# First mixer of a two-block transformer: projections, delta rule and attention in another order, with the residual put away in DRAM

## The chip, the core and the metric

The kernel runs on one core of one Trainium2 chip. The metric is the device time of one execution in microseconds (us); lower is better. TensorE multiplies 128x128 weights with up to 512 columns into PSUM, VectorE (DVE), ScalarE (ACT) and GpSimd (POOL) do the elementwise work, and DMA queues on SyncE (SP), ScalarE and GpSimd move data. Each engine works through its own instructions strictly in the order in which the program lists them; semaphores tie the engines together.

## The reference

The program is two blocks of a transformer on 512 tokens of width 1024. The change touches only the mixer of the first block. It computes two branches from one normalised input and one projection matrix `w_in`:

```python
proj = h @ w_in                      # 1024 -> qkv_a 1536 | z_a 512 | a, b 16 | qkv_b 1536
# branch a: gated delta rule, 4 heads of 128, forward and backward
qkv = silu(short_conv(qkv_a, conv_w))            # 5 taps along the tokens
q, k, v = l2_normalize(q), l2_normalize(k), v
lmat = strict_lower(kb @ k.T * decay)            # per chunk and head
tmat = inverse(eye + lmat)                       # triangular solve
u, w = tmat @ (v * beta), tmat @ (kb * exp(g))
for chunk: v_new = u - w @ state; o = qg @ state + intra @ v_new
           state = state * exp(gl) + kdec.T @ v_new
o_a = rms_norm(o_fwd + o_bwd) * silu(z_a)
# branch b: banded attention, 8 heads of 64, with a bias by distance
o_b = softmax(rms_norm(q_b) @ rms_norm(k_b).T + bias) @ v_b
x = x + concat(o_a, o_b) @ w_out
```

Before the mixer stands a feed-forward block, behind it another; then the second transformer (two layers) follows.

## The kernel before

Everything is kept with features on the 128 partitions and the 512 tokens along the free dimension. A projection of 128 output features is one weight block: 512 KB come by DMA into one of three `raw` buffers, ScalarE rounds them into `wh`, VectorE puts the rest into `wl` (two buffers of each), and TensorE issues 8 x 3 products `xl·wh`, `xh·wl`, `xh·wh` of 512 columns (`projF`, through `mm3`), 24 per block. `w_in` makes 28 blocks: 12 for the convolved q, k, v of the delta rule (tiles `pqkv`, from which `pad` is cut and `cv` is made by five taps; blocks 0 to 7 are q and k and are normalised by `row_scales` and `row_apply`, 8 to 11 are v), 8 for q and k of attention (`psw`, normalised and stored to DRAM as `qkd`), 4 for v of attention (`psv`, turned into `sV`) and 4 for the gate z (`psz`). `w_out` makes 8 more (`pwo`).

Between these stands the delta rule: matrices `B` and `IT` by head and direction (`pkk`, `pqk`, `pgr`), a triangular inverse of the 32x32 diagonal blocks on VectorE alone (31 pairs of instructions on `dX` and `dT`; the blocks reach it through DRAM as `dg`, `dgd`, `dM`, and leave it through `dgi` to `dR`), two levels that widen the inverse to 128x128 (`unit`: masks `bl` by GpSimd, `py`, copies `ys`, `pa`, `pb`), and the recurrence over four chunks for eight heads and directions (`psc`, `vn`, `pso`). Attention works on 32 items, one head and 128 queries each: scores `pS`, bias and maximum on VectorE, exponential `P`, transposition `ptp`, copy `PT`, product `po`, scaled into `Y`. `prepare(h)` fetches K and Q of a head from `qkd`, splits them on ScalarE and GpSimd and fetches its bias `bq` with GpSimd's queue; `bq` shares two buffers with `dM` and `dT`.

The source is written as one program, and a list scheduler places the instructions of each engine when the program is built, under the limits of buffers and PSUM banks. PSUM's eight banks are two pools of four, `acc` (projections) and `mx` (the rest). Lines that the text speaks of: L244 is every matmul, L250 and L262 elementwise work, L269 and L272 ScalarE, L623 the bias fetch, L631 the fetch `T<-qkd`.

Of the kernel before, what the change touches and what calls it, by code (L numbers as in the profile page):

```python
# [9 lines left out]
F32 = mybir.dt.float32  # L10
F32R = mybir.dt.float32r
# [7 lines left out]
NT = 512  # L19
# [186 lines left out]


class Builder:
    def __init__(self, tc, A, out, taps=None, stop=None):
# [102 lines left out]

    def wget(self, kk=8):
        nc = self.nc
        n = 128 * kk * 128
        src = self.w_ap[self.w_off:self.w_off + n].rearrange("(p x) -> p x", p=128)
        self.w_off += n
        with self.tc.high_priority():
            raw = self.ps_w.tile([128, 8, 128], F32, tag="raw", name="raw", bufs=3)
            h = self.ps_w.tile([128, 8, 128], F32R, tag="wh", name="wh", bufs=2)  # L320
            l = self.ps_w.tile([128, 8, 128], F32R, tag="wl", name="wl", bufs=2)
            nc.sync.dma_start(out=raw[:, :kk].rearrange("p k n -> p (k n)"), in_=src)
            self.acopy(h[:, :kk], raw[:, :kk])
            self.sub(l[:, :kk], raw[:, :kk], h[:, :kk].bitcast(F32))
        return h, l
# [12 lines left out]

    def projF(self, XH, XL, c0, n, name):

        h, l = self.wget()
# [5 lines left out]
    def projV(self, XH, XL, toks, name):  # L347

        c0, n = min(c for c, _ in toks), sum(k for _, k in toks)
        t = self.slab("sT", "vt")  # L350
        for ps, s in self.projF(XH, XL, c0, n, name):
            self.acopy(t[:, s], ps)
        return t
# [436 lines left out]
    def mixer1(self):  # L790
# [60 lines left out]
        def conv(m, _):  # L851
            pad = self.slab("sT", "pad")
            nc.gpsimd.memset(pad[:, 0:2], 0.0)
            nc.gpsimd.memset(pad[:, 514:516], 0.0)
            for ps, s in self.projF(XH, XL, MT, NT, "pqkv"):
# [10 lines left out]
            if m < 8:  # L866
                self.act(cv, cv, AF.Silu)
            return cv

        def sums(m, cv):  # L870
            if m >= 8:
                self.act(cv, cv, AF.Silu)
            return cv, self.row_scales(cv, chunks, 128, 1.0, self.mx) if m < 8 else None

        def rest(m, got):
            cv, y = got
            if m < 8:
                self.row_apply(cv, y, chunks, 128, 128 ** -0.5 if m < 4 else 1.0, self.mx)
            else:
                pt = self.mx("pvt")  # L880
# [14 lines left out]
        dgs = [self.slab("u", "dg", width=NT) for _ in range(2)]  # L895
        cc = [slice(128 * c, 128 * c + 128) for c in range(4)]
        by_c = lambda a: a.rearrange("p (c t) -> p c t", t=128)
        for h in range(4):
# [4 lines left out]
            for d in range(2):  # L903
# [44 lines left out]
        for d in range(2):  # L948
            for x in range(4):
                src = d2[32 * x + 16 * d:32 * x + 16 * d + 16, :].rearrange("u (r c) -> r u c", c=32)  # L950
                eng = nc.sync if x % 2 else nc.scalar
                eng.dma_start(out=R[d][32 * x:32 * x + 32, :].rearrange("p (u c) -> p u c", c=32), in_=src)
            nc.vector.transpose(out=Rt[d], in_=R[d])


# [118 lines left out]

        sw = self.small("sw", 1)
        self.ts(sw, self.v("qn"), 0.125, ALU.mult)
        qkd = self.ps_dram.tile([8, 128, NC], F32, name="qkd")

        def proj(i, _):
            group = []  # L1080
            for m in (2 * i, 2 * i + 1):
                t = self.slab("y" if m % 4 == 3 else "sT", "sT")
                for ps, s in self.projF(XH, XL, MT, NT, "psw"):
                    self.mul(t[:, s], ps, rs[:, s])
                group.append(t)
            return group

        def sums(i, group):
            return group, self.group_scales(group, SEQ, 64, 1.0 / 64, self.acc)

        def normed(i, got):
            for m, t, y in zip((2 * i, 2 * i + 1), *got):
                self.row_apply(t, y, SEQ, 64, sw if m < 4 else self.v("kn"), self.acc)
                nc.gpsimd.dma_start(out=qkd[m, :, S], in_=t[:, S])

        staged(4, proj, sums, normed)
        V = [self.slab("V", "sV", width=NT) for _ in range(4)]
        staged(4, lambda m, _: self.projV(XH, XL, toks, "psv"), lambda m, t: self.turnV(
            t, toks, lambda i, ps: self.act(V[i][:, cc[m]], ps, AF.Copy, scale=rsc[:, i:i + 1]), self.acc))


        Yh, Yl = [None] * 8, [None] * 8
        heads = {}

        def prepare(h):
            p, x = divmod(h, 2)
            r = slice(64 * x, 64 * x + 64)
            K = self.stackK(qkd[4 + p, r, :], S, ("sT", "u"), False)
            Q = self.stackQ(qkd[p, r, :], S, ("sT", "u"), False)
            heads[h] = {"K": K, "Q": Q, "Y": heads[h - 1]["Y"] if x else self.slab("y", "Y", width=NT),  # L1110
# [3 lines left out]
        def scores(i, _):  # L1114
# [19 lines left out]
        def turn(i, P):  # L1134
            T = self.slab("u", "PT", width=NT)
            pt = self.mx("ptp")
            for cs in cc:
                self.tr(pt[:, cs], P[:, cs])
            self.acopy(T, pt)
            return T  # L1140

        def product(i, T):
# [3 lines left out]
            z = slice(t, t + 1)  # L1146
            po = self.mx("po")
            for j, cs in enumerate(cc):
# [3 lines left out]
            if t == 3 and x:  # L1152
                Yh[4 + p], Yl[4 + p] = self.slab("u", "Yh", F32R), self.slab("u", "Yl", F32R)

# [4 lines left out]

                self.to_features(by_c(u["Y"]), None, sink, self.mx)  # L1160

        zs = [None] * 4

        def gate(m):
            zs[m] = z = self.slab("z" if m < 3 else "u", "z")
            for ps, s in self.projF(XH, XL, MT, NT, "psz"):
                self.mul(z[:, s], ps, rs[:, s])

# [9 lines left out]

        def step(i, _):
            if i in (2, 7, 12, 17):  # L1180
                gate((i - 2) // 5)
            if i in (20, 22, 24, 26):
                gated((i - 20) // 2)
            return scores(i, _)
# [553 lines left out]

    nu = 32

# [69 lines left out]
```

## Time and profile before

| | before |
|---|---|
| time, median of 3 runs | 3395.32 us (3391.58 to 3395.39) |
| time of the profiled execution | 3389.28 us |
| its span | 3387.5 us |
| granted TensorE clock, mean of the span | 0.956 |
| TensorE busy | 3264.6 us, 96% of the span |
| VectorE, ScalarE, GpSimd busy | 51%, 34%, 14% |
| the first mixer in the span | about 400 to 877 us |

Busy shares say in how much of the time an instruction was in the engine. A granted clock of 1.00 is 2.4 GHz and 0.50 is 1.2 GHz; values between are means over a stretch. In the rows, `[8.31 <-POOL Q L250]` says that the engine was idle for 8.31 us until the GpSimd instruction of line 250 that writes `Q` was done.

### The profile page before, as it was taken

What the parts mean: (1) busy time and instruction counts of PE and PEld (TensorE: products, weight loads), DVE (VectorE), ACT (ScalarE), POOL (GpSimd) and SP (SyncE); (2) the same over time, 40 slices, a digit from 0 to 9 for tenths busy, and PEclk for the clock granted to TensorE, in tenths of its full rate; (3) what the DMA queues carried; (4) which work ended last, traced back from release to release, by engine and by line L of the source; (5) the groups of instructions that cost most, each with busy time, mean ns of one, the idle gap of its engine ahead of it and who ended that gap; (6) DMA issues with size and microseconds to landing.
All of it is one profiled execution on the core that took longest, in us unless ns stands there. A gap on an engine that the chain in (4) does not pass through costs nothing.

```text
span 3387.5 us, 47666 instructions
## 1 busy us (share of the span) xinstructions
PE 3264.6 (96%) x18886; PEld 2816.5 (83%) x18886; DVE 1716.5 (51%) x3632; ACT 1145.1 (34%) x1958; POOL 480.9 (14%) x575
## 2 busy tenths in 40 slices
PE   8999989998999999999899999999999799999998
PEld 6778778876888889998898899999888688788886
DVE  4443378563544355544674744433665374654433
ACT  4222343365322233212553232222322363232221
POOL 1010010422000013321220400000342221400000
PEclk9999999998999999888998999999998898899999
DMA  3333223332333233123332522223323342523332
GB/s 127 103 106 115 87 63 106 101 96 65 93 94 94 91 112 109 60 79 103 116 117 72 164 88 90 92 95 124 97 78 95 115 126 94 165 87 97 94 94 77
DMA packets 121271, 337.26 MB, mean 100 GB/s; under 512 B 28853, under 2 KB 29248, under 8 KB 121048
## 3 DMA queue, kind: packets, MB, share of 16 engines
q1 hardware_dynamic: 87656, 267.95, 25.5%
q0 software_dynamic: 21712, 54.51, 5.2%
q10 hardware_dynamic: 11680, 11.76, 1.1%
q8 instruction: 148, 2.42, 0.3%
q14 instruction: 75, 0.61, 0.1%
HBM read 298.42 MB, written 39.56 MB: 100 GB/s over the span
## 4 chain that ended last, share of the span: by engine, by line
PE 55%; DMA 3%; DVE 2%; issue 2%; POOL 1%; ACT 1%; POOLq 0%; SPq 0%; DVEq 0%; ACTq 0%
PE pgz L244 11%; PE pd L244 7%; PE pg L244 7%; PE pu L244 7%; PE po L244 4%; PE pwo L244 3%; PE pA L244 2%; PE pqk L244 2%; DMA T<-qkd 2%; PE pod L244 2%; PE pdz L244 1%; PE pS L244 1%; PE pT L244 1%; PE pbr L244 1%; PE pdi L244 1%
## 5 line engine op out<-in xcount | busy, mean ns | idle before, releaser
L272 ACT CAST wh<-raw 128x1024 fp32r<-128x1024 f32 (+1 forms) x448 | 463.6, 1035 | 1532.1 <-issue 722.7
L250 DVE TENSOR_TENSOR wl<-raw,wh 128x1024 fp32r<-128x1024 f32 (+1 forms) x448 | 555.4, 1240 | 425.8 <-ACT wh L272 425.2
L244 PE MATMUL pg<-xl,wh 128*128 128x512 f32 (+1 forms) x880 | 283.3, 354 | 13.2 <-DVE xl L262 13.2
L244 PE MATMUL pg<-xh,wh 128*128 128x512 f32 (+1 forms) x880 | 282.4, 353 | 0.0
L244 PE MATMUL pu<-xl,wh 128*128 128x512 f32 (+1 forms) x880 | 281.3, 352 | 0.0
L244 PE MATMUL pd<-hl,wh 128*128 128x512 f32 (+1 forms) x880 | 281.1, 352 | 0.0
L244 PE MATMUL pu<-xh,wh 128*128 128x512 f32 (+1 forms) x880 | 281.0, 352 | 0.0
L244 PE MATMUL pd<-hh,wh 128*128 128x512 f32 (+1 forms) x880 | 280.8, 352 | 0.0
L244 PE MATMUL pg<-xh,wl 128*128 128x512 f32 (+1 forms) x880 | 280.5, 351 | 0.0
L244 PE MATMUL pu<-xh,wl 128*128 128x512 f32 (+1 forms) x880 | 279.7, 350 | 0.0
L244 PE MATMUL pd<-hh,wl 128*128 128x512 f32 (+1 forms) x880 | 278.5, 349 | 0.0
L244 PE MATMUL pgz<-xl,wh 128*128 128x264 f32 (+1 forms) x768 | 222.9, 341 | 0.0
L244 PE MATMUL pgz<-xh,wh 128*128 128x264 f32 (+1 forms) x768 | 218.0, 334 | 0.0
L244 PE MATMUL pgz<-xh,wl 128*128 128x264 f32 (+1 forms) x768 | 217.5, 333 | 0.0
L250 DVE TENSOR_TENSOR fb<-pu,rs 128x512 f32<-128x512 f32 (+1 forms) x110 | 62.6, 586 | 290.6 <-PE pu L244 290.6
L244 PEld LDWEIGHTS pg<-xl,wh 128*128 128x128 f32 x880 | 153.8, 189 | 38.6 <-DVE xl L262 15.4
L244 PEld LDWEIGHTS pu<-xh,wl 128*128 128x128 f32 x880 | 153.9, 188 | 27.3 <-issue 2.6
L244 PEld LDWEIGHTS pg<-xh,wl 128*128 128x128 f32 x880 | 154.5, 189 | 26.3 <-issue 1.7
L244 PEld LDWEIGHTS pg<-xh,wh 128*128 128x128 f32 x880 | 154.9, 189 | 25.2 <-issue 0.9
L244 PEld LDWEIGHTS pu<-xh,wh 128*128 128x128 f32 x880 | 154.3, 189 | 24.8 <-issue 0.9
L244 PEld LDWEIGHTS pd<-hh,wl 128*128 128x128 f32 x880 | 153.9, 188 | 24.9
L244 PEld LDWEIGHTS pd<-hh,wh 128*128 128x128 f32 x880 | 153.6, 188 | 24.4
(487 smaller groups left out, 6521.9 us busy)
## 6 DMA issues: line engine op xcount, KB each, us to landing
raw<-in_win SPq DMA_DIRECT2D x136, 512.0 KB
raw<-in_gu SPq DMA_DIRECT2D x88, 512.0 KB
raw<-in_f1gu SPq DMA_DIRECT2D x44, 512.0 KB
raw<-in_f2gu SPq DMA_DIRECT2D x44, 512.0 KB
raw<-in_dn SPq DMA_DIRECT2D x32, 512.0 KB
raw<-in_wout SPq DMA_DIRECT2D x24, 512.0 KB
gates<-g POOLq DMA_DIRECT2D x32, 264.0 KB, 2.6
gr<-gates SPq DMA_DIRECT2D x32, 264.0 KB
```

The lines of the kernel that those rows point to most:

```text
L244: return self.nc.tensor.matmul(out=out, lhsT=lhsT, rhs=rhs, start=start, stop=stop)
L250: return (eng or self.nc.vector).tensor_tensor(out=out, in0=a, in1=b, op=op)
L272: return self.nc.scalar.copy(out=out, in_=in_)
```

## The change

The residual `X` (eight tiles) is stored to DRAM after the mixer's norm and fetched again ahead of the output projection; in its room a pool of eight slabs, `at1`, is opened for attention (heads 0 to 3; later heads use the slabs of the normalised input). Attention takes its PSUM from `acc` instead of `mx`. Weight blocks are fetched by number instead of in the order of the file. The projections are written in another order: q and k of attention go between the convolutions of q and k and the heads' matrices (`staged_steps`, `next(first)`), and v of attention, the convolutions of v and all four gates behind the inverse and ahead of the two levels. The gate's last step (`gated`) moves behind the 32 items. `nu`, the number of general slabs, goes from 32 to 31.

```diff
+def staged_steps(n, *steps):
+    got = [None] * n
+    for i in range(n + len(steps) - 1):
+        for j, step in enumerate(steps):
+            if 0 <= i - j < n:
+                got[i - j] = step(i - j, got[i - j])
+        yield i
...
-    def wget(self, kk=8):
+    def wget(self, kk=8, blk=None):
         n = 128 * kk * 128
+        if blk is not None:
+            self.w_off = blk * n
...
         XH, XL, rs, rsc = self.norm(toks, "mix")
-        self.open("m1", {"V": 4, "u": self.nu, "sT": 5, "y": 2, "z": 3})
+        self.spill_x(slice(0, NC))
+        self.open("at1", {"at": 8}, side="right")
+        self.open("m1", {"V": 4, "u": self.nu, "sT": 5, "y": 2, "z": 4})
...
-        staged(12, conv, sums, rest)
-        q, k, vt = C[0:4], C[4:8], C[8:12]
+        first = staged_steps(4, proj, sums2, normed)
+        for i, _ in enumerate(staged_steps(8, conv, sums, rest)):
+            if i in (3, 7):
+                next(first)
+        q, k, vt = C[0:4], C[4:8], [None] * 4
         for h in range(4):
             pk, pq = self.mx("pkk"), self.mx("pqk")
...
+            next(first)
...
+        staged(4, lambda m, _: self.projV(XH, XL, toks, "psv", 20 + m), turnV)
+        staged(4, value, lambda m, cv: cv, lambda m, cv: cv, value_turned)
+        for m in range(4):
+            gate(m)
         def unit(u):
...
-            P = self.slab("u", "P", width=NT)
-            ps = self.mx("pS")
+            P = self.slab(tag(h), "P")[:, :NT]
+            ps = self.acc("pS")
...
-        staged(32, step, lambda i, P: P, turn, product)
+        staged(32, scores, lambda i, P: P, turn, product)
+        for h in range(4):
+            gated(h)
...
+        self.close("at1")
+        self.fill_x(slice(0, NC))
         self.out_proj("wout1", Yh, Yl, MT, NT, range(8))
```

The scheduler makes of this the following orders. On TensorE, where the two levels begin, the order before was (`psv` is v of attention; `py`, `pa`, `pb` are the levels):

```order
L244 MATMUL psv<-xl,wh 128x512
L244 MATMUL psv<-xh,wl 128x512
L244 MATMUL py<-n_3969,bl 128x128 x4
L244 MATMUL psv<-xh,wh 128x512
L244 MATMUL py<-n_3975,bl 128x128 x4
L244 MATMUL pa<-n1t,ys 128x128 x4
L244 MATMUL pb<-ys,n1t 128x128 x4
```

In the changed program the levels stand behind all 96 products each of `psv`, of the four v convolutions (`pqkv`) and of `psz`. These rows are TensorE's at the end of the v convolutions; the row of 16 transposes is `cv` of v turned, four per convolution:

```order
L254 MATMUL pqkv<-xl,wh 128x512
L254 MATMUL pqkv<-xh,wl 128x512
L254 MATMUL pqkv<-xh,wh 128x512
L257 MATMUL pvt<-ct,cv 128x128 x16
L254 MATMUL psz<-xl,wh 128x512
L254 MATMUL psz<-xh,wl 128x512
```

So the gates now wait behind the transposes of v, and the levels behind the gates. On ScalarE the same place, from the fetch of the inverse (`dR<-dgi`) to the copies `vt` of the turned v, reads in the changed program:

```order
L282 CAST wh<-raw 128x1024
L1001 DMA dR<-dgi 32x16x32 x2
L282 CAST wh<-raw 128x1024
L1001 DMA dR<-dgi 32x16x32 x2
L279 ACTIVATE cv<-pad,vc 128x512
L279 ACTIVATE tap<-pad,vc 128x512 x4
L279 ACTIVATE cv<-pad,vc 128x512
L279 ACTIVATE tap<-pad,vc 128x512
L279 ACT_TABLE_LOAD
L279 ACTIVATE cv<-cv 128x512
L279 ACTIVATE tap<-pad,vc 128x512 x3
L279 ACTIVATE cv<-pad,vc 128x512 x2
```

The taps of the v convolutions 8 and 9, which before stood among the convolutions of q and k, now stand behind the fetch of the finished inverse. On GpSimd the order before was, from those taps to the first masks of the levels:

```order
L250 TENSOR_TENSOR cv<-cv,tap 128x512 x8
L919 DMA itd<-IT 128x4x128 x8
L1094 DMA qkd<-sT 128x512 x4
L623 DMA bq<-bper_575 128x1x896
L1094 DMA qkd<-sT 128x512
L623 DMA bq<-bper_575 128x1x896
L1094 DMA qkd<-sT 128x512 x2
L250 TENSOR_TENSOR bl<-B,ct 128x512 x2
```

and in the changed program:

```order
L260 TENSOR_TENSOR K_5658<-T,K_5657 64x512
L260 TENSOR_TENSOR Q_5663<-T,Q_5663 64x512
L635 DMA bq<-bper_575 128x1x896 x2
L260 TENSOR_TENSOR cv<-cv,tap 128x512 x8
L260 TENSOR_TENSOR bl<-B,ct 128x512 x5
L1047 DMA ntd<-n1t 128x4x128 x2
L260 TENSOR_TENSOR bl<-B,ct 128x512
L260 TENSOR_TENSOR K_5683<-T,K_5682 64x512
```

The eight additions of the taps now stand behind two fetches of `bq`, whose two buffers are those of `dM` and `dT`, and K and Q of the first heads are split among the masks of the levels.

## Rows read from the trace of the kernel before

**Rows 1.** Busy time by stretch: length, PE, PEld, DVE, ACT, POOL, PEclk, DMA, GB/s
```profile
441.00:548.00 107.00, 98.65 (x556) 84.92 (x557) 92.34 (x257) 49.88 (x90) 17.19 (x30) 0.94 0.24 74
548.00:608.00 60.00, 54.26 (x257) 45.88 (x255) 43.43 (x140) 17.38 (x26) 7.43 (x11) 0.80 0.49 125
608.00:660.00 52.00, 47.85 (x364) 44.75 (x365) 31.96 (x42) 12.86 (x22) 25.07 (x23) 0.97 0.16 55
660.00:705.00 45.00, 44.28 (x327) 40.23 (x326) 29.54 (x104) 27.53 (x88) 8.57 (x16) 1.00 0.40 132
705.00:785.00 80.00, 70.29 (x366) 52.77 (x366) 35.67 (x132) 57.13 (x115) 20.08 (x21) 0.94 0.30 90
785.00:840.00 55.00, 46.02 (x261) 36.30 (x261) 16.35 (x57) 28.33 (x68) 12.13 (x17) 0.84 0.17 50
840.00:877.00 37.00, 36.93 (x158) 29.47 (x158) 21.64 (x28) 15.42 (x22) 0.00 (x0) 1.00 0.33 100
```

**Rows 2.** TensorE by tile, `psw` to 551 us and `psv` to 608 us: ns, starts
```profile
L244 PE MATMUL psw<-xl,wh x32: 388/392/479, 507.3 to 550.1; 128*128 128x512 f32 x32
...
L244 PE MATMUL psv<-xl,wh x7: 389/628/735, 599.3 to 606.8; 128*128 128x512 f32 x7
```

**Rows 3.** TensorE in order of time, two neighbouring products: start, length
```profile
507.62 0.39 PE L244 MATMUL psw<-xh,wl 128*128 128x512 f32 x1
507.85 0.40 PE L244 MATMUL psw<-xh,wh 128*128 128x512 f32 x1
```

**Rows 4.** TensorE in order of time, attention without fill, from scores to next scores
```profile
734.59 0.90 PE L244 MATMUL pS<-K,Q 128*128 128x512 f32 x2
...
736.73 0.90 PE L244 MATMUL pS<-K,Q 128*128 128x512 f32 x2
```

**Rows 5.** VectorE in order of time: taps of a convolution; last step of the inverse
```profile
441.82 6.04 DVE L262 SCALAR_TENSOR_TENSOR cv<-pad,vc,cv 128x512 f32<-128x512 f32 x9
...
592.50 0.19 DVE L250 TENSOR_TENSOR dT<-dT,dX 128x31 f32<-128x31 f32 x1
```

**Rows 6.** GpSimd in order of time, with the waits ahead of each
```profile
480.90 10.66 POOL L250 TENSOR_TENSOR cv<-cv,tap 128x512 f32<-128x512 f32 x8 [6.59 <-ACT tap L269]
...
596.41 0.54 POOL L623 DMA_DIRECT2D bq<-bper  x1 [0.53 <-DMA dgi<-dT]
...
775.86 1.27 POOL L250 TENSOR_TENSOR Q<-T,Q 64x512 fp32r<-64x512 f32 x1 [0.19 <-ACT Q L272]
...
804.20 1.26 POOL L250 TENSOR_TENSOR Q<-T,Q 64x512 fp32r<-64x512 f32 x1
```

**Rows 7.** ScalarE's groups, 440 to 515 us: busy us, mean ns, idle before
```profile
L269 ACT ACTIVATE cv<-pad,vc 128x512 f32<-128x512 f32 x12 | 8.4, 716 | 9.8 <-DVE pad L250 6.1 <-DVE yh L275 2.0 <-DVE ry L262 1.5
L269 ACT ACTIVATE cv<-cv 128x512 f32<-128x512 f32 x12 | 7.5, 628 | 14.2 <-DVE cv L262 14.2
```

**Rows 8.** ScalarE's groups, 705 to 785 us
```profile
L269 ACT ACTIVATE P<-P,rsnm 128x512 f32<-128x512 f32 x19 | 13.7, 721 | 2.2 <-DVE rsrec L1150 1.3 <-DVE rsnm L266 0.8
L272 ACT COPY PT<-ptp 128x512 f32<-128x512 f32 x18 | 10.4, 576 | 6.9 <-PE ptp L247 6.9
L269 ACT ACT_TABLE_LOAD x8 | 10.3, 1283 | 0.1
L272 ACT CAST wh<-raw 128x1024 fp32r<-128x1024 f32 x5 | 5.2, 1045 | 1.1 <-PE psv L244 0.5 <-PE psz L244 0.4
```

**Rows 9.** TensorE's first products of the levels, and of head 6
```profile
608.59 1.13 PE L244 MATMUL py<-n,bl 128*128 128x128 f32 x8 [1.16 <-DVE n L250]
...
805.51 1.51 PE L244 MATMUL pS<-K,Q 128*128 128x512 f32 x2 [8.31 <-POOL Q L250]
```

**Rows 10.** TensorE alone by stretch: length, busy, granted clock, DMA, GB/s
```profile
800.00:810.00 10.00, 4.49 (x15) 0.50 0.21 62
810.00:820.00 10.00, 10.00 (x46) 0.68 0.01 2
```

**Rows 11.** The second block's store of the residual, by tile: ns, starts
```profile
L552 ACTq DMA_DIRECT2D xd<-x x16: 326/327/1088, 1264.8 to 2352.6; - x16
```

More of the change, by code (lines that the diff above doesn't have):

```diff
@@ L345, in projF, with projV @@
         return outs
-    def projV(self, XH, XL, toks, name):
+    def projV(self, XH, XL, toks, name, blk=None):
         c0, n = min(c for c, _ in toks), sum(k for _, k in toks)
         t = self.slab("sT", "vt")
-        for ps, s in self.projF(XH, XL, c0, n, name):
+        for ps, s in self.projF(XH, XL, c0, n, name, blk):
             self.acopy(t[:, s], ps)
@@ L854, in conv @@
             nc.gpsimd.memset(pad[:, 514:516], 0.0)
-            for ps, s in self.projF(XH, XL, MT, NT, "pqkv"):
+            for ps, s in self.projF(XH, XL, MT, NT, "pqkv", m):
                 self.mul(pad[:, 2:514], ps, rs[:, s])
@@ L865, in conv @@
                     self.add(cv, cv, t, nc.gpsimd)
-            if m < 8:
-                self.act(cv, cv, AF.Silu)
+            self.act(cv, cv, AF.Silu)
             return cv
         def sums(m, cv):
-            if m >= 8:
-                self.act(cv, cv, AF.Silu)
             return cv, self.row_scales(cv, chunks, 128, 1.0, self.mx) if m < 8 else None
@@ L879, in rest @@
             else:
-                pt = self.mx("pvt")
+                pt = self.acc("pvt")
                 for c in range(4):
@@ L886, in rest, with proj, sums2, normed @@
             C[m] = cv
-        staged(12, conv, sums, rest)
-        q, k, vt = C[0:4], C[4:8], C[8:12]
+        sw = self.small("sw", 1)
+        self.ts(sw, self.v("qn"), 0.125, ALU.mult)
+        qkd = self.ps_dram.tile([8, 128, NC], F32, name="qkd")
+        def proj(i, _):
+            group = []
+            for m in (2 * i, 2 * i + 1):
+                t = self.slab("sT", "sT")
+                for ps, s in self.projF(XH, XL, MT, NT, "psw", 12 + m):
+                    self.mul(t[:, s], ps, rs[:, s])
+                group.append(t)
+            return group
+        def sums2(i, group):
+            return group, self.group_scales(group, SEQ, 64, 1.0 / 64, self.acc)
+        def normed(i, got):
+            for m, t, y in zip((2 * i, 2 * i + 1), *got):
+                self.row_apply(t, y, SEQ, 64, sw if m < 4 else self.v("kn"), self.acc)
+                nc.gpsimd.dma_start(out=qkd[m, :, S], in_=t[:, S])
+        V = [self.slab("V", "sV", width=NT) for _ in range(4)]
+        def turnV(m, t):
+            self.turnV(t, toks, lambda i, ps: self.act(V[i][:, cc[m]], ps, AF.Copy, scale=rsc[:, i:i + 1]), self.acc)
+        zs = [None] * 4
+        def gate(m):
+            zs[m] = z = self.slab("z", "z")
+            for ps, s in self.projF(XH, XL, MT, NT, "psz", 24 + m):
+                self.mul(z[:, s], ps, rs[:, s])
+        cc = [slice(128 * c, 128 * c + 128) for c in range(4)]
+        first = staged_steps(4, proj, sums2, normed)
[3 more added lines that the diff above has]
+        q, k, vt = C[0:4], C[4:8], [None] * 4
         B = {}
@@ L895, in mixer1 @@
         dgs = [self.slab("u", "dg", width=NT) for _ in range(2)]
-        cc = [slice(128 * c, 128 * c + 128) for c in range(4)]
         by_c = lambda a: a.rearrange("p (c t) -> p c t", t=128)
@@ L953, in mixer1, with value, value_turned @@
             nc.vector.transpose(out=Rt[d], in_=R[d])
+        def value(m, _):
+            cv = conv(8 + m, None)
+            return cv
+        def value_turned(m, cv):
+            rest(8 + m, (cv, None))
+            vt[m] = C[8 + m]
+        staged(4, lambda m, _: self.projV(XH, XL, toks, "psv", 20 + m), turnV)
+        staged(4, value, lambda m, cv: cv, lambda m, cv: cv, value_turned)
+        for m in range(4):
+            gate(m)
         def unit(u):
@@ L1072, in mixer1 @@
             self.mul(o3, o3, sy.unsqueeze(2).to_broadcast([128, 4, 128]))
[L1075 to L1099, printed above, removed]
         Yh, Yl = [None] * 8, [None] * 8
         heads = {}
+        tag = lambda h: "at" if h < 4 else "xn"
         def prepare(h):
@@ L1134, in turn @@
         def turn(i, P):
-            T = self.slab("u", "PT", width=NT)
-            pt = self.mx("ptp")
+            T = self.slab(tag(i // 4), "PT")[:, :NT]
+            pt = self.acc("ptp")
             for cs in cc:
@@ L1152, in product @@
             if t == 3 and x:
-                Yh[4 + p], Yl[4 + p] = self.slab("u", "Yh", F32R), self.slab("u", "Yl", F32R)
+                Yh[4 + p], Yl[4 + p] = (self.slab("xn" if p < 2 else "u", n, F32R) for n in ("Yh", "Yl"))
                 def sink(ps, s):
@@ L1158, in sink @@
                     self.split(Yh[4 + p][:, s], Yl[4 + p][:, s], t[:, s], nc.gpsimd)
[L1160 to L1167, printed above, removed]
+                self.to_features(by_c(u["Y"]), None, sink, self.acc)
         def gated(h):
```

18 lines of the change are left out of this document (6 added, 12 removed).

## The prediction, written before the changed kernel ran

> **What bounds the kernel now.** I read the table of busy time by stretch first [rows 1]. The reader is to see that TensorE is busy in nearly all of it, and that the first mixer, 400 to 877 us, is where it is least so. A busy TensorE still says little, since neighbouring products overlap: they start 0.23 us apart and are shown 0.39 long [rows 3]. So I count products at 0.2325 us (a block of 24 is 5.58) and set that against the clock time. In the order of time next: one attention item without fill takes 736.73 - 734.59 = 2.14 us of TensorE [rows 4]. Then the waits. TensorE has 54.3 us busy in the 60 from 548 to 608, at a clock of 0.80; 46.0 in the 55 from 785 to 840, at 0.84, and there it once waits 8.31 us for Q of head 6 [rows 1, 9]. After that wait the clock is 0.50 to 810 and 0.68 in the next ten [rows 10]: half rate for 4.5 + 6.4 = 10.9 us, which costs 5.4 us of products. So some 60 us of the mixer are waits and half rate; the change can only move these, since no product is added or removed.
>
> **The change part by part.** The sum is made against the profiled execution, 3389.3 us, whose mixer ends at 877 with its last product; that execution is 6.0 us below the median of the runs, 3395.3.
>
> *To the end of the heads' matrices (I).* By 551 us TensorE has now done all 288 products of `pqkv` and 96 of the 192 of `psw` [rows 2]: 384. In the new order 192 of `pqkv` and 192 of `psw` stand there, the same 384. VectorE, 92.3 us busy in 107 [rows 1], loses eight taps at 0.67 (6.04 / 9) [rows 5] and four `pad`, and gains the norms of all `psw`, about equal work. What comes in on TensorE (norms of `psw`, 64 small products and sums, 9 us by their starts) stands against what goes: GpSimd's eight additions [rows 6] leave this stretch. I take 551 again, bounds 543 and 560.
>
> *Inverse (II).* Behind 551 stand now `psv` 96, v convolutions 96, `psz` 96. The first two and 16 transposes: 551 + 8 x 5.58 + 2 = 597.6. Then the 16 transposes of `cv`, all before `psz`. When is `cv` there? The last pairs of `dX` and `dT` stand behind the `pad` of the second v convolution, at 586.5, and I give them 4 us: 590.5. The result reaches DRAM 3.9 us later (592.5 to 596.4 now [rows 5, 6]): 594.4. ScalarE, ahead of the taps, must also round a weight block (1.05 [rows 8]) whose buffer comes free at 597.6, and issue the fetches: 599.7. Then `cv` and four taps, `cv` and one tap at 0.716 [rows 7], a table load of 1.28 [rows 8]: 606.0. GpSimd's four additions at 1.27 (10.66 / 8 with overlap [rows 6]) end by 606.5; the Silu (0.63 [rows 7]), three taps and two `cv` follow: 610.7. Only then can VectorE do the eight taps of convolutions 10 and 11: 5.4, then a Silu and the last transposes: 618. So TensorE stands from 597.6 to 618 but for 2.5 us of transposes: **a new wait of about 18 us**. Then `psz`, 22.3, and a restart at half rate as at 805 [rows 10], 5.4: the levels begin at 645.7, where they began at 608.6 [rows 9]. Bounds of the wait: 8 us, if the fetches don't hold ScalarE, and 24.
>
> *Levels and rule (III, IV).* Now 608 to 705, 97 us [rows 1]. Of `psv`'s 96 products about 20 are done by 608 [rows 2]; the other 76 leave (17.7 us), with 2 us of transposes. In come about 13 attention items by the order, 13 x 2.14 = 27.8. TensorE is nearly full there (47.9 of 52, 44.3 of 45 [rows 1]), so I count all: 105 us, to 750.7. Bounds 97 and 127 (rival C).
>
> *Attention alone (V).* 19 items stand behind the rule's last product: 40.7, and 3.5 of transposes of `Y` and `O`. GpSimd still fetches and copies `uq` between Q of head 5 and Q of head 6 (28 us apart now [rows 6]), with less to fill the time: I keep the 8.3 us wait and 5.4 of half rate [rows 9, 10], and 9 for short waits in the pipeline, in the proportion of 805 to 840. 67 us, to 817.7; bounds 55 and 75. In this stage table loads go: eight stand in 705 to 785, 10.3 us [rows 8], since Silu of z lay between exponentials; one is left. By the row that frees 9.0 us of ScalarE, which I count as the cover of its other work. The Trainium skill, "ScalarE: Activation LUTs", section "What ACT_TABLE_LOAD costs", puts a switch at 2.66 us with a drain; by that, 18.6 us would come free. The row shows no idle beside 0.1 us, so the row's price stands.
>
> *Tail and output projection (VI).* The order puts the casts of the gated heads behind the last `Y`, and the first product waits for them: 4 us. Then all 192 products of `pwo` stand alone, 44.7 and 1.3 for the start: to 867.7. Now only some 158 / 192 of them remain at 840 [rows 1].
>
> *The residual in DRAM.* Sixteen DMAs, issued by ScalarE in 0.33 us each (up to 1.09 [rows 11]); eight stand in the feed-forward's last stage and eight in V, under TensorE's products. I count zero; if ScalarE is the bound in V, 4 us. The weights keep their rate: the DMA share there is 0.17 to 0.49 [rows 1].
>
> The sum: 551.0 + 94.7 + 105 + 67 + 4 + 46 = 867.7, against 877: 9.3 us less. That is 3380.0 for the profiled execution, or **3386** from the median. A measurement of this kernel can tell about 0.2%, 6.8 us, from no change.
>
> **The rivals.**
>
> *B, the fill lands.* The v convolutions are ready when the transposes come, so II has neither the wait nor the half rate: 18 + 5.4 less, 3363. For it: `pad` of these convolutions is ready long before, and the stretch 548 to 608 has room on ScalarE (17.4 of 60 [rows 1]). Against: both engines take their orders in turn, and the taps stand behind the fetch of the inverse.
>
> *C, the other side: the items hold up the levels and the rule.* `P` (0.72), `PT` (0.58 [rows 8]) and two splits of 1.27 [rows 6] now stand among the copies `ys` and the masks `bl`, and each level waits for its own. Two items and one head for each of the four pairs of units make 4 x (2.6 + 2.5) = 20 us, with 2 more in the rule: 3386 + 22 = 3408. It decides once III and IV last over 121 us instead of 105. For it: the levels' first product already waited 1.16 us on VectorE [rows 9], and such waits take the clock along: 0.50 after 805 [rows 10]. The Trainium skill, "TensorE: Matmul & The Clock Gate", section "HAM oscillation — how this bites in real kernels", says the same of bursts parted by waits: each burst starts again at half rate; the trace agrees in these two rows.
>
> *D, nothing to be measured.* The list scheduler already drew `psw` and `psv` into the rule before the change [rows 2], so the new order only exchanges fills: 3395.
>
> **How the numbers follow.** The forecast has 0.42, B 0.26, C 0.22, D 0.10. The forecast's own range is 3376 to 3395, of which I put 0.26 below the bound of 0.2% and 0.16 within it. B is all faster; of C 0.20 is slower and 0.02 within; of D 0.06 is within and 0.02 on either side. Faster 0.54, same 0.24, slower 0.22. The range goes from somewhat beyond B, 3358, to C, 3408.
>
> **What would show it.** In the new trace: (1) TensorE at the end of the heads' matrices at 551, give or take 8. (2) A wait of TensorE at the transposes of `cv`, some 18 us, ended by ScalarE, then a stretch at 0.50; if it is under 8, B is right. (3) The first `py` near 646. (4) From there to the rule's last product 105 us; over 121, C is right. (5) A wait at head 6's first scores, some 8 us. (6) Unbroken `pwo` of 45 us. The prediction is wrong if the first two stages end far from 646, which rests on one chain of ScalarE and GpSimd, or if the pipeline of attention runs much slower than 2.14 us an item beside the rule.

## The result, and the profile after

The change made the kernel slower. Its median is 3413.87 us in 5 runs (3410.13 to 3428.67), beside 3393.35 us for the kernel before on the same chip (3389.25 to 3395.39); the ratio is 1.0067, with a 95% interval of 1.0046 to 1.0088. That lies 28 us over the forecast and above the range.

The profiled execution, 3428.67 us (span 3426.9, mean clock 0.946), is the longest of the five. Its mixer ends with its last output product at 900.0, where that of before ends at 876.8: 23.2 us of the difference. The other 16 us lie behind the mixer, where both programs issue the same instructions in the same order. The other four executions took 3410 to 3416 us and were not profiled; that most of these 16 us are missing there is inferred from their times alone. So the text speaks of the mixer alone. Its stages stand in the table of busy time by stretch, cut where the stages now begin (columns as in [rows 1]):

```profile
441.00:561.00 120.00, 115.73 (x672) 101.62 (x672) 88.40 (x296) 48.56 (x88) 8.47 (x20) 0.93 0.24 80
561.00:615.00 54.00, 51.31 (x218) 39.20 (x217) 37.56 (x92) 17.47 (x35) 5.80 (x15) 0.95 0.35 98
615.00:649.00 34.00, 4.20 (x18) 3.18 (x17) 14.06 (x17) 13.89 (x21) 13.49 (x12) 0.54 0.49 129
649.00:673.00 24.00, 24.00 (x103) 19.46 (x102) 6.64 (x9) 5.62 (x9) 1.76 (x1) 0.94 0.27 87
673.00:784.00 111.00, 101.84 (x764) 92.61 (x763) 70.03 (x178) 58.01 (x154) 46.29 (x50) 0.94 0.30 92
784.00:850.00 66.00, 62.38 (x325) 49.20 (x323) 28.06 (x137) 37.22 (x93) 15.37 (x23) 0.74 0.25 70
850.00:900.00 50.00, 46.61 (x194) 37.46 (x195) 24.93 (x31) 18.77 (x27) 1.28 (x1) 0.97 0.26 80
```

Two columns tell where the 23 us went, as sums over the rows. Idle time of TensorE (length less busy) is 52.9 us in these seven rows and 37.7 in [rows 1]: 15 more. Busy time multiplied by what is missing from a clock of 1.00 is 37.8 us here and 29.8 in [rows 1]: 8 more. Most of the added idle time is in the third row, 34 us with 4.2 of work. Most of the missing clock is in the sixth, attention alone at 0.74, where the last stretch of attention before had 0.84 over fewer microseconds.

Now the same execution in order of time, engine by engine (start, length, what it is, the wait ahead of it):

```profile
547.83 1.86 PE L254 MATMUL pss<-ct,sq 128*128 128x2 f32 x8 [2.52 <-ACT sq L279]
...
636.68 1.12 PE L257 MATMUL pvt<-ct,cv 128*128 128x128 f32 x4 [21.46 <-ACT cv L279]
642.38 1.12 PE L257 MATMUL pvt<-ct,cv 128*128 128x128 f32 x4 [4.58 <-ACT cv L279]
647.25 1.97 PE L257 MATMUL pvt<-ct,cv 128*128 128x128 f32 x8 [3.76 <-ACT cv L279]
...
672.52 1.95 PE L254 MATMUL py<-n,bl 128*128 128x128 f32 x16
...
813.18 1.52 PE L254 MATMUL pS<-K,Q 128*128 128x512 f32 x2 [2.37 <-POOL Q L260]
...
600.79 0.62 ACT L282 CAST K<-T 128x512 fp32r<-128x512 f32 x1 [7.61 <-DMA T<-qkd]
...
612.87 0.62 ACT L282 CAST Q<-T 128x512 fp32r<-128x512 f32 x1 [9.28 <-DMA T<-qkd]
613.39 1.05 ACT L282 CAST wh<-raw 128x1024 fp32r<-128x1024 f32 x1
627.13 0.94 ACTq L1001 DMA_DIRECT2D dR<-dgi  x2
...
576.63 0.21 DVE L260 TENSOR_TENSOR dX<-dM,dT 128x31 f32<-128x31 f32 x1 [3.74 <-DMA dM<-dgd]
...
602.39 1.47 DVE L260 TENSOR_TENSOR wl<-raw,wh 128x1024 fp32r<-128x1024 f32 x1 [3.56 <-ACT wh L282]
...
609.70 0.19 DVE L260 TENSOR_TENSOR dT<-dT,dX 128x31 f32<-128x31 f32 x1
...
614.93 0.49 SPq L643 DMA_DIRECT2D T<-qkd  x1
...
615.98 0.42 SPq L995 DMA_DIRECT2D dgi<-dT  x1
```

The waits at `pvt<-ct,cv` are 21.46 + 4.58 + 3.76 = 29.8 us. Behind them is a chain over four engines, read from below. The inverse's first step is at 576.63, when its blocks `dM` have come back from DRAM, and its last at 609.70. Its store `dgi` leaves SyncE only at 615.98, since a fetch of attention (`T<-qkd`, 614.93) and a weight block stand ahead of it on that queue, and lands 11.1 us later, when ScalarE can issue `dR` (627.13). The taps of the v convolutions stand behind that. One thing in these rows the prediction had not listed: the casts `K<-T` and `Q<-T` are those of attention's head 0. The list scheduler drew its fetches up into the inverse; ScalarE waited 7.61 and 9.28 us for them, with the rounding of weight blocks behind it, and with that VectorE (3.56 us, in the middle of the inverse).

The fetches are not the whole of the delay. In the kernel before, the inverse's first step stood 20 us earlier:

```profile
556.63 0.20 DVE L250 TENSOR_TENSOR dX<-dM,dT 128x31 f32<-128x31 f32 x1
```

The blocks leave for DRAM in two stores (`dgd<-dg`, on SyncE), the second with the last of the heads' matrices. That second store was issued at 544.2 before and at 566.1 now: before, products of `psw` still followed the matrices (to 581), and now the matrices come last in their stage, which itself ends ten us later. From its first step the inverse then took 35.9 us before and 33.1 now.

### The profile page after: what moved, and what is told of

Same layout as the page of the kernel before. It is cut to its first block, busy times and chain, and to the rows that moved or that the text cites. A ratio compares the mean times of both kernels' runs of the same rounds, so it can differ in the third digit from the quotient of the medians.

```text
span 3426.9 us, 47655 instructions
## 1 busy us (share of the span) xinstructions
PE 3288.7 (96%) x18886; PEld 2840.0 (83%) x18886; DVE 1713.0 (50%) x3632; ACT 1136.5 (33%) x1952; POOL 482.6 (14%) x575
## 4 chain that ended last, share of the span: by engine, by line
PE 55%; DMA 2%; DVE 2%; issue 1%; ACT 1%; POOL 1%; SPq 0%; POOLq 0%; DVEq 0%; ACTq 0%
PE pgz L254 11%; PE pg L254 7%; PE pu L254 7%; PE pd L254 7%; PE po L254 4%; PE pwo L254 3%; PE pA L254 2%; PE pqk L254 2%; PE pod L254 2%; DMA T<-qkd 2%; PE pdz L254 1%; PE pS L254 1%; PE pT L254 1%; PE pbr L254 1%; PE pdi L254 1%
```

## The experiments

Each kernel ran in five rounds against the kernel before on the same chip; there before had 3396 to 3399 us. "Last `pwo`" is the end of the mixer's last output product in the profiled execution (before 876.8, after 900.0). It is one execution for each kernel, and the mixer's first product starts between 398.2 and 400.1 in them, so differences under 2 us in this column are not read. The intervals of x1, x2, x6, x9 and x10 overlap that of the change: what they gain on it is read from these single executions. Those of x3 and x11 lie below it, those of x4 and x5 above.

| run | what it is | ratio to before | last `pwo` |
|---|---|---|---|
| after | the change | 1.0067 (1.0046 to 1.0088) | 900.0 |
| x1 | after, head 0 and 1 fetched late | 1.0045 (1.0026 to 1.0063) | 893.8 |
| x2 | after, v convolutions early | 1.0050 (1.0035 to 1.0065) | 889.9 |
| x3 | after, gates ahead of v convolutions | 1.0025 (1.0010 to 1.0040) | 878.7 |
| x4 | projections' part alone | 1.0207 (1.0191 to 1.0223) | 941.2 |
| x5 | x4 and 96 more products | 1.0110 (1.0091 to 1.0128) | 916.4 |
| x6 | after, gates back in attention | 1.0055 (1.0036 to 1.0073) | 897.2 |
| x7 | attention's part alone | 1.0100 (1.0085 to 1.0116) | 909.5 |
| x8 | x7, two `psw` steps early | 1.0061 (1.0048 to 1.0074) | 896.5 |
| x9 | after and 48 more products | 1.0046 (1.0030 to 1.0062) | 893.8 |
| x10 | x1 and x2 | 1.0045 (1.0030 to 1.0059) | 889.7 |
| x11 | x10 and x9 | 1.0028 (1.0016 to 1.0039) | 880.5 |
| x12 | x7, attention in the old banks | 1.0007 (0.9994 to 1.0020) | 876.9 |
| x13 | x12 and 24 more products | 0.9996 (0.9983 to 1.0008) | 875.2 |
| x14 | x12, one `psw` step early, gates at items 8 to 20 | 1.0033 (1.0021 to 1.0045) | 892.1 |
| x15 | x13, one `psw` step early | 1.0053 (1.0037 to 1.0069) | 898.3 |

The first theory, "late inverse", was that the loss is the wait at `pvt`, and that the wait is long because the inverse came late. Its rivals: "lost cover" (the inverse takes its time wherever the rest stands, so the idle time only moves), and "attention" (the loss is in attention's own part).

**x1, the fetches of heads 0 and 1 wait for the inverse.**

```diff
         t = self.slab(tag, "T")
+        if late is not None:
+            self.vcopy(t[0:1, s.start:s.start + 1], late[0:1, 0:1])
...
+            late = Rt[1] if h < 2 else None
```

> The fetches of the queries and keys of attention's heads 0 and 1 (T<-qkd) are made to wait for the inverse's result by one element written into their tile; nothing else changes. Late-inverse theory (the inverse itself came late because these fetches stand ahead of its own steps: the head-0 casts K<-T and Q<-T made ScalarE wait 7.61 and 9.28 us, the weights' split behind them held VectorE's dT chain 3.56 us, dgi was issued 6 us after the last dT and landed 11 us after its issue against 3.3 us before): dR lands near 609 instead of 627, the taps of the v convolutions follow at once, the waits ahead of the transposes pvt<-cv fall from 29.8 us to 10 to 15, and the time to 3394 to 3402 us. Lost-cover theory (the inverse ends when its serial VectorE chain ends, wherever fetches stand): at most the 3.6 us of the held split come back, the waits stay above 22 us, 3410 to 3415 us. Attention theory (the loss lies in attention beside the rule and its half clock after it): no change, 3414.

In order of time, TensorE's waits and ScalarE:

```profile
622.32 1.12 PE L257 MATMUL pvt<-ct,cv 128*128 128x128 f32 x4 [8.41 <-ACT cv L279]
628.02 1.12 PE L257 MATMUL pvt<-ct,cv 128*128 128x128 f32 x4 [4.58 <-ACT cv L279]
639.03 1.97 PE L257 MATMUL pvt<-ct,cv 128*128 128x128 f32 x8 [9.89 <-ACT cv L279]
...
632.66 0.62 ACT L282 CAST K<-T 128x512 fp32r<-128x512 f32 x1 [4.22 <-DMA T<-qkd]
```

`dR` now starts at 611.6 instead of 627.1: 4.3 us from an earlier last `dT` (605.42), 6.0 from `dgi` leaving at once, 5.2 from its landing in 5.9 us instead of 11.1. So the fetches did make the inverse late, by 15.5 us. But `dR` started at 596.0 before, and the other half of the delay, the inverse's late start, is still there (first step at 574.93). And the casts of head 0, released with the inverse, now stand between the v convolutions on ScalarE (4.22 and 4.07 us of waiting), and the third wait grew to 9.89. The sum is 22.9 us, between the two theories' numbers. Of 15.5 us won, 9 are left at the first `py` (663.8) and 6 at the end. The time, 1.0045 of before, is not clear of the change's 1.0067.

**x2, the v convolutions back among q and k.**

```diff
-        for i, _ in enumerate(staged_steps(8, conv, sums, rest)):
+        for i, _ in enumerate(staged_steps(12, conv, sums, rest)):
...
-        staged(4, value, lambda m, cv: cv, lambda m, cv: cv, value_turned)
```

> The four v convolutions go back among the q and k convolutions, as in the kernel before; all else as in the changed kernel. Late-inverse theory: no wait at pvt<-cv; the heads' matrices end 22 us later, the v and z projections (about 47 us) lie under the inverse, and at the first py at most some 10 us of wait are left, so first py near 645 instead of 672.5 and 3385 to 3397 us. Lost-cover theory: the idle time only moves from pvt<-cv to the first py, 20 us or more there, first py near 660 to 670, 3403 to 3414 us. Attention theory: the stages behind first py stay as they are; what the levels gain is kept, but at least half of it is lost again at the half clock, 3403 or more.

The waits at `pvt` are gone, and one of 22.40 us has come up, at the first transposition of attention, which the scheduler put ahead of the levels; `P` waits on ScalarE behind `dR`:

```profile
666.03 1.11 PE L257 MATMUL ptp<-ct,P 128*128 128x128 f32 x4 [22.40 <-ACT P L279]
...
679.47 3.75 PE L254 MATMUL py<-n,bl 128*128 128x128 f32 x16 [1.82 <-DVE n L260]
```

This is the lost-cover theory's number, though not at its place. Both theories missed the first `py`: it comes at 679.47, 7 us later than in the changed kernel, and yet the mixer ends 10 us earlier, since attention items have run ahead of it.

**x3, the gates ahead of the v convolutions.**

```diff
-        staged(4, value, lambda m, cv: cv, lambda m, cv: cv, value_turned)
         for m in range(4):
             gate(m)
+        staged(4, value, lambda m, cv: cv, lambda m, cv: cv, value_turned)
```

> The four gate projections psz are issued ahead of the v convolutions instead of behind them; nothing else changes. Late-inverse theory (products wait at pvt<-cv only because the convolutions' taps stand behind the inverse on ScalarE, GpSimd and VectorE, and there is no work left for TensorE): 22 us of products now lie in that wait, the waits at pvt<-cv fall from 29.8 to about 8 to 12 us, first py near 652, 3391 to 3400 us. Lost-cover theory: the v convolutions' products come 22 us later and so do their taps (18 us of them), so the wait stays near 20 us or more and the gain is under 8 us, 3406 to 3414 us. Attention theory: no change beyond 5 us.

```profile
634.08 0.79 PE L254 MATMUL pqkv<-xh,wl 128*128 128x512 f32 x1 [4.85 <-DVE wl L260]
...
652.33 1.11 PE L257 MATMUL pvt<-ct,cv 128*128 128x128 f32 x4 [3.90 <-ACT cv L279]
659.25 1.11 PE L257 MATMUL pvt<-ct,cv 128*128 128x128 f32 x4 [5.81 <-ACT cv L279]
660.02 2.22 PE L254 MATMUL pS<-K,Q 128*128 128x512 f32 x3
662.03 3.56 PE L254 MATMUL py<-n,bl 128*128 128x128 f32 x16
```

The waits at `pvt` fell to 3.90 + 5.81 = 9.7 us, as the late-inverse theory said, and the mixer ends 21 us earlier, within 2 us of that of before. So some 20 us hung on the order of two statements. But the first `py` is at 662.0, not at 652: ten of the 21 us are won there. TensorE now waits 5.9 us, in two places, for weight blocks of the v convolutions, 4.85 of them for `wl` on VectorE. Some 7 of the 21 us are won in attention, which runs from the rule's last product to the first `pwo` in 62 us instead of 69.5, at a granted clock of 0.83 in 766 to 830. Why the clock is higher there was not tested. The ratio, 1.0025, is a little above the 3391 to 3400 us expected.

**x4, the projections' part alone.**

```diff
-        self.open("at1", {"at": 8}, side="right")
-        tag = lambda h: "at" if h < 4 else "xn"
+        tag = lambda h: "u"
...
-            ps = self.acc("pS")
+            ps = self.mx("pS")
```

> The projections' part of the change alone: attention takes its tiles and PSUM banks from the shared pools again, the residual stays in SBUF, the fourth gate lies in the shared pool. Attention theory: with attention's part gone the loss is gone, 3395 or less. Late-inverse and lost-cover theories: the wait at pvt<-cv stays (20 to 30 us: one of the three early fetches of attention is still ahead of dgi), the levels and the rule run without attention in them (about 92 us instead of 111), and all 32 items of attention follow alone (about 100 us instead of 66), 3408 to 3425 us.

Both theories were far off: 2.07% slower. The stage of attention shows why. Busy time by stretch, then one item to the next:

```profile
760.00:800.00 40.00, 35.68 (x119) 25.98 (x120) 18.93 (x81) 18.71 (x43) 11.79 (x10) 0.50 0.20 65
800.00:840.00 40.00, 40.00 (x148) 31.25 (x147) 9.34 (x40) 19.05 (x48) 10.19 (x13) 0.50 0.21 65
840.00:880.00 40.00, 40.00 (x147) 31.25 (x146) 9.39 (x41) 19.61 (x49) 9.22 (x15) 0.50 0.12 34
```

```profile
773.39 1.50 PE L254 MATMUL pS<-K,Q 128*128 128x512 f32 x2
...
777.29 1.50 PE L254 MATMUL pS<-K,Q 128*128 128x512 f32 x2
```

All 32 items ran at 1.2 GHz, 3.90 us apart instead of 2.14 [rows 4], with no wait of TensorE over 1.6 us to be seen after the first (5.65 us for `Q`). In the kernel before, `psz` and the first `pwo` stand among the items. This made a new theory, "clock": those dense products hold TensorE at 2.4 GHz through attention, and the change took them away. Its rival, "latency", is that an item is a chain through VectorE and ScalarE, and the clock a consequence.

**x5, x4 with more work.**

```diff
+            for _ in range(3):
+                self.mm(ps, u["Q"][:, i0:i0 + 128], K1[:, S])
             self.mm(ps, u["Q"][:, i0:i0 + 128], K1[:, S], True, False)
```

> The kernel of x4 with more work: each first score product of attention (pS, 128x512) is made four times, the first three overwritten by the last one's start flag, so the output is unchanged and TensorE has 96 more products of 512 columns. In x4 the 32 items of attention took 762.7 to 891.7 us at a granted clock of 0.50 with TensorE busy throughout. Clock theory (attention without dense products beside it keeps TensorE at the half clock, and this, not its work, is what the moved projections cost): the added products bring the clock back, items cost 2.14 + 0.70 us at full clock, attention takes 90 to 97 us instead of 129, and the time falls from 3471 to about 3430 to 3442 us, though there is more work. Latency theory (an item's length is the chain through VectorE and ScalarE, the clock a consequence): attention is no shorter, or longer by the products, 20 to 40 us, 3470 to 3510 us.

```profile
780.00:820.00 40.00, 39.26 (x240) 29.95 (x239) 13.61 (x56) 26.25 (x67) 11.02 (x11) 1.00 0.29 88
820.00:860.00 40.00, 39.23 (x238) 29.52 (x237) 13.17 (x54) 25.21 (x63) 14.82 (x22) 1.00 0.21 65
```

3434.4 us instead of 3471.4, with 96 products more (on another chip, where before had 3396.5 and not 3399.2); 240 matmuls in 40 us instead of 148. The 5.66 us wait ahead of the first item is still there, so the wait is not what keeps the clock down. The latency theory is out.

**x6, the gates back in attention.**

```diff
+            if i in (16, 19, 22, 25):
+                gate((16, 19, 22, 25).index(i))
+            if i in (24, 26, 28, 30):
+                gated((24, 26, 28, 30).index(i))
             return scores(i, _)
```

> The changed kernel with the four gate projections psz back among the attention items (at items 16, 19, 22, 25) and the gated outputs at items 24 to 30, as the kernel before had them; heads 4 to 7 take the shared slabs, since the projections still read the normed input. The v convolutions stay behind the inverse. Clock theory: the stretch of attention behind the rule runs at full clock; psz's 24 us leave the place ahead of the levels (first py 649 instead of 672.5) and come back in attention, where half clock cost 15 to 20 us: pwo begins 12 to 22 us sooner than 853.6 and the ratio to before falls from 1.0067 to 1.000 to 1.003. Latency theory: psz only moves and what is won ahead of the levels is paid in attention, ratio 1.005 to 1.008.

```profile
760.00:820.00 60.00, 57.02 (x299) 44.66 (x297) 30.51 (x106) 39.29 (x77) 18.00 (x25) 0.91 0.40 113
820.00:850.00 30.00, 25.86 (x104) 21.37 (x104) 7.26 (x27) 16.20 (x35) 1.27 (x1) 0.56 0.06 18
```

The clock is 0.91 while `psz` lasts (to 815.5) and 0.56 behind it. The first `py` comes at 652.0, 20 us sooner, but the first `pwo` only 3 us sooner (850.5, where the clock theory had 12 to 22), and the ratio, 1.0055, is in the latency theory's range. By the clock column it is the stretch behind `psz` that takes the gain back, and so something else had kept the clock up at the end of the kernel before.

**x7, attention's part alone, and x12, the same in the old banks.** x7 is the kernel before with the residual in DRAM and attention in slabs and banks of its own; x12 takes the banks back.

```diff
-            ps = self.acc("pS")
+            ps = self.mx("pS")
...
-            po = self.acc("po")
+            po = self.mx("po")
```

> Attention's part of the change alone, on the kernel before: residual in DRAM meanwhile, attention with its own eight slabs and the other PSUM banks; all projections and gates as in the kernel before. If the loss is the projections' (both theories above): faster than before, since the wait of 8.31 us ahead of head 6 and the half clock behind it (5 us) go: ratio 0.996 to 0.998, 3380 to 3391 on a chip where before is 3395. If attention's own part carries the loss: ratio over 1.002.

> x7 with attention's products back in the shared PSUM banks; residual in DRAM and own slabs stay. In x7 no output projection (pwo) stood among the last attention items, where the kernel before has some 40 of them, and the clock was 0.50 from 800 to 862. If the banks keep pwo away (clock theory): pwo products stand among the last items again, the clock there is over 0.9 for most of it, and the ratio falls from 1.0100 to 0.997 to 1.002. If the residual's way through DRAM or the slabs carry x7's loss: 1.006 or more.

First x7, by stretch and the output projection by tile; then x12, the same:

```profile
740.00:800.00 60.00, 49.88 (x236) 37.69 (x235) 17.83 (x53) 34.27 (x65) 11.17 (x11) 0.87 0.32 101
800.00:860.00 60.00, 58.59 (x218) 45.85 (x218) 16.01 (x60) 29.86 (x71) 12.10 (x19) 0.50 0.09 26
...
L244 PE MATMUL pwo<-Yl,wh x64: 388/395/775, 862.5 to 908.7; 128*128 128x512 f32 x64
```

```profile
780.00:800.00 20.00, 19.27 (x70) 14.51 (x70) 4.81 (x17) 9.48 (x23) 6.70 (x12) 0.50 0.35 106
800.00:840.00 40.00, 40.00 (x244) 32.05 (x243) 14.03 (x51) 24.44 (x59) 9.76 (x12) 0.94 0.15 41
...
L244 PE MATMUL pwo<-Yl,wh x64: 388/395/775, 802.4 to 876.1; 128*128 128x512 f32 x64
```

x7's expectation was wrong: attention's part alone costs 1.0%. With its own banks attention shares `acc` with the output projection, whose first product now comes at 862.5, behind the last item; 60 us of attention run at 0.50. In the old banks `pwo` begins at 802.4 among the items and the clock is 0.94 from there. The ratio falls to 1.0007: DRAM and slabs cost nothing that can be measured, the banks all of it.

**x8, x14, x15, the change's early `psw` in x7 and x12.** x8 issues two of four steps inside the convolutions, x14 and x15 one. x14 also puts the gates at items 8 to 20, where x12, x13 and x15 have them at 2 to 17. So the clean pairs are x8 with x7 and x15 with x13.

```diff
+        for i, _ in enumerate(staged_steps(12, conv, sums, rest)):
+            if i in (5, 9):
+                next(first)
```

> x7 with two of the four psw steps issued inside the convolutions (as the changed kernel does) and the other two left behind the heads' matrices: psw and psv stay as the inverse's cover, psz is left to fill the levels, the rule and attention. Clock theory: the gap at the convolutions (6.23 us and 3 us of lower clock) and the head-6 wait both go, no new wait: ratio 0.992 to 0.997. Latency theory: less psw is left for the inverse (45 us of products were there before, some 40 with psv now), so a wait of 10 us or more comes up ahead of the first py and eats it: 0.998 to 1.003.

> x12 with one of the four psw steps issued inside the convolutions, as the changed kernel does (the rest stay behind the heads' matrices), and the gates at items 8 to 20. If the gap there (6.22 us ahead of pn at 490, clock 0.74) is worth its fill: 6 to 9 us less by the heads' matrices, the inverse still covered by psw and psv, pwo ends at 868 to 873, ratio 0.996 to 0.999. If the cover is needed more at the inverse: a wait of 5 us or more before the first py and half clock behind it, ratio 1.000 to 1.003.

> x14 (gates as in the kernel before) with x13's added products in heads 4 and 5. If both are right and independent: ratio 0.994 to 0.998; if the earlier psw leaves attention's first heads without gate products beside them: half clock in heads 2 and 3 and 1.000 or more.

All missed the better outcome. Against x7, x8 is faster (1.0061 and 1.0100); against x13, x15 is slower (1.0053 and 0.9996). As in the changed kernel, a step of `psw` ahead of the heads' matrices makes the inverse start later (572.4 in x15, 556.4 in x13), and the first `py` with it (624.1 and 606.3). With `psw` gone from behind the heads' matrices, `psv` takes its place under the inverse and `psz` is drawn into the levels and the rule, so that attention lacks it: 0.50 from 800 to 840 in x8, from 780 to 820 in x14, from 760 to 800 in x15. Nor did the step fill the gap in the convolutions in x14, whose wait is 4.66 us where before has 6.23. Fill put in at one end came out at the other, at the half clock; how much of the loss is the later inverse and how much the clock was not separated.

**x9, x11, x13, more products where the clock is low; x10, x1 and x2 together.** x9 repeats the score product as in x5, for heads 4 to 7 of the changed kernel, x13 for heads 4 and 5 of x12; x11 is x9's edit on x10.

```diff
+            for _ in range(3 if h > 3 else 0):
+                self.mm(ps, u["Q"][:, i0:i0 + 128], K1[:, S])
```

> The changed kernel with the first score product of attention's heads 4 to 7 made four times (48 more products of 512 columns, 11 us at full clock; the output is unchanged). In the changed kernel the granted clock was 0.50 from 815 to 845. Clock theory: it stays near 1.00 there, the items take 2.84 us instead of up to 4, the last po ends at 838 to 845 instead of 849.2 and the ratio to before falls from 1.0067 to 1.003 to 1.006, with more work. Latency theory: the stretch gets longer by the added products, 11 us or more, ratio 1.010 or more.

> x1 and x2 together: the v convolutions among the others, and the fetches of heads 0 and 1 after the inverse. In x2 the first transposes of attention (ptp) stood ahead of the levels on TensorE and waited 22.4 us for an exponential that stood behind the inverse on ScalarE; with the late fetch they stand behind the levels' start. If that order is what kept x2's gain away: the first py waits under 10 us and comes near 645 to 655 instead of 679.5, ratio 0.997 to 1.002. If the inverse's own length is what counts (lost-cover theory): 15 us or more of wait ahead of the first py, which comes at 660 or later, ratio 1.003 to 1.006.

> x10 with the 48 added products of x9. Clock theory: 3 to 10 us under x10, full clock to the end of attention; with it the best version of the changed kernel, ratio 0.994 to 1.000. Latency theory: 11 us or more over x10.

> x12 with the first score product of heads 4 and 5 made four times (24 more products of 512 columns, 5.6 us at full clock; the output is unchanged). In x12 the granted clock was 0.50 in 780 to 800, between the last gate product and the first output projection. Clock theory: it is 0.9 or more there, 9 us come back for 5.6 spent: pwo ends 2 to 6 us before x12's 876.9, ratio 0.998 to 1.000. Latency theory: 5 us longer, ratio 1.002.

The changed kernel and x9 in the same two stretches:

```profile
800.00:820.00 20.00, 17.47 (x97) 13.40 (x96) 8.59 (x30) 11.30 (x29) 9.20 (x17) 0.80 0.45 127
820.00:840.00 20.00, 20.00 (x74) 15.37 (x73) 4.64 (x21) 9.41 (x24) 2.54 (x2) 0.50 0.10 28
```

```profile
800.00:820.00 20.00, 20.00 (x126) 15.25 (x125) 8.11 (x31) 12.59 (x33) 7.91 (x16) 1.00 0.56 159
820.00:840.00 20.00, 20.00 (x128) 15.59 (x128) 7.39 (x28) 12.16 (x30) 3.84 (x3) 1.00 0.15 42
```

The clock is 1.00 throughout and the ratio 1.0046, within what the clock theory said and well under the latency theory's 1.010; that x9 is faster than the change is not clear of noise. The last `po` of x9 ends at 843.3 instead of 849.5, though its first `py` came 0.8 us later. x11 is below x10 (1.0028 and 1.0045, intervals that overlap; the last `pwo` 9 us sooner), but over its forecast. In x10 the order is mended, and the first `py` comes at 652.1, as forecast, but what waits there is the inverse itself:

```profile
652.10 3.76 PE L254 MATMUL py<-n,bl 128*128 128x128 f32 x16 [11.13 <-DVE n L260]
668.16 3.78 PE L254 MATMUL pa<-n1t,ys 128*128 128x128 f32 x16 [6.69 <-ACT ys L282]
```

x10's 20 us won at the first `py` shrink to 10 at the end: the second wait is ScalarE's, and attention's last 49 us run at 0.56 to 0.65. Its ratio, 1.0045, is in the lost-cover theory's range. x13 is the best of all, 0.9996, and not to be told from the kernel before or from x12; the clock in 780 to 800 rose from 0.50 to 0.84, under the 0.9 expected. No version beat the kernel before.

## Why the prediction was wrong

By its own list of what would show it:

1. *End of the heads' matrices, 551 ± 8.* It was 561.3, outside the bounds. The count of products was right, their place was not. The last `psw` stands at 535.8, and the matrices of the last two heads run on to 557.7 with no projection beside them: a wait of 2.52 us, and 0.76 in 548 to 561.
2. *A wait of 18 us at the transposes of `cv`, ended by ScalarE, then half clock.* The mechanism was right, the size was not: 29.8, beyond the bound of 24. **The step that failed is the one in stage II that asks when `cv` is there**: it put the last `dT` at 590.5, and it was 609.70. Ten of these 19 us come from stage I. x1 gives 4.3 of the rest to the early fetches. The other 4.6 are the inverse itself: the prediction dated its end by the `pad` that stand among its steps and did not ask when it can begin. It begins when `dM` is back, and took 30.5 us from there even in x1 (574.93 to 605.42). Behind `dT`, issue and landing of `dgi` took 6.3 + 11.1 us where the prediction took 3.9; x1 gives 11 of that to the same fetches. It followed `prepare` only in the attention stage and did not look for its fetches on the queues of the inverse.
3. *First `py` near 646.* 672.5, from 1 and 2. x3 shows that 22 us of gate products cover two thirds of the wait at `pvt`, but bring the first `py` only to 662.0.
4. *Levels and rule 105 us.* 111; under 121, so rival C was not it, though the time came out 6 us from C's 3408. Rival D's ground was in part misread: `psw` had ended by 581 before, under the inverse, and only `psv` reached the levels and the rule.
5. *A wait of 8 us at head 6.* 2.37. Attention alone still took 66 us against 67, so this term was right in its sum and wrong in its parts: the half clock, priced at 5.4, lost 62.38 x 0.26 = 16 us.
6. *Unbroken `pwo` of 45 us.* 46.4, as forecast. But the prediction priced it as a mere move. x7 and x12 show what it cost: the output projections had held the clock among the last items.

Points 1 to 3 make the sum wrong by 27 us, and stage III and IV by 6; the mixer ended 32 us later than forecast. Behind these stands a wrong premise, "the change can only move these, since no product is added or removed". Waits were moved and grew, and the half clock is not conserved: x5 has more products than x4 and takes some 35 us less.

What the runs attribute: the banks cost 0.93% in the order of before (x7 against x12). In the changed order the gates' place costs some 20 us of the mixer (x3). The early fetches cost some 5 (x1). The half clock of attention's last heads costs at least 5, for x9 won that after paying for some 11 us of added products. These overlap: x3 already raised the clock of attention, and x3 was not tried together with x1 and x9. The projections' part alone costs 2.07% (x4), of which x5 won back 1.0% by keeping the clock. So attention's part costs 1.0% in the old order (x7) and is worth 1.4% in the new one (after against x4): it mends part of what the projections' part breaks.

The Trainium skill, "TensorE: Matmul & The Clock Gate", section "HAM oscillation — how this bites in real kernels", ties the half rate to waits between short bursts of products. The trace agrees in 615 to 649, where TensorE waits and the clock is 0.54. In x4 it goes further than the page: 40.00 us busy of 40, and 0.50.

## What to carry to other kernels

Work that fills a stage may also be what holds TensorE's clock there, as in x12 against x7. Before moving dense products out of a stage of transposes and narrow products, look at the granted clock of a like stretch without them and price all the remaining work at the lower level; the PSUM pool that a stage uses can decide which fill stands beside it, as it did in x7. And where work is moved ahead of a round trip through DRAM, list what every in-order queue holds in that stretch, the fetches of later stages that a scheduler draws forward among them.

## What was not expected of the hardware

Adding 96 products of 128x512 to x4 brought the clock of its attention stage from 0.50 to 1.00 and the kernel from 3471.4 to 3434.4 us. At 0.50 the rows showed TensorE busy without a gap, so a full busy column did not show the clock. A store of 512 KB (`dgi`) landed in 3.3 us before, 5.9 in x1 and 11.1 after, with fetches of attention on the same queue in the last; why it took longer was not measured by itself.
